# Another order of work from the softmax to the first expert in a hybrid encoder layer

## The chip, the cores and the metric

The kernel runs on one core of one Trainium2 chip. The metric is device time in microseconds (us) of one execution, lower is better. All engines of the core work side by side, each through its own list of instructions in order, and wait for one another with semaphores: PE (TensorE, matrix multiplication; PEld is its loading of weights), DVE (VectorE), ACT (ScalarE), POOL (GpSimd), and SP (SyncE), which only issues transfers from device memory.

## What is computed

One encoder layer over 256 tokens of width 1024: attention and a gated recurrence side by side, one output projection, then a mixture of 32 experts of which each token takes 4. All data are float32. Cut to what the change touches:

```python
mixed = jnp.concatenate([rms_norm(attn, attn_out_g[l]),
                         rms_norm(lru, lru_out_g[l])], axis=-1)
x = x + mixed @ w_out[l]                      # output projection, both halves
x = x + moe_ffn(rms_norm(x, norm2_g[l]), w_router[l], ...)
...
# moe_ffn
logits = (xf @ w_router + b_router)
top_v, top_i = lax.top_k(logits, TOP_K)       # 4 of 32
gates = jax.nn.softmax(top_v, axis=-1)
counts = jnp.bincount(flat_e, length=N_EXPERTS)
...
def expert_block(args):                       # rows of the tokens that chose expert e
    g = xb @ w_gate[e] + b_gate[e]
    u = xb @ w_up[e] + b_up[e]
    ...
    return ((u + 1.0) * glu) @ w_down[e] + b_down[e]
```

## The kernel before

The program has two parts, `front` (attention, recurrence, output projection, router) and `experts` (a loop over 32 experts). Nothing reorders the work: each engine runs its instructions in the order in which the Python code writes them, so the order of the code is the schedule.

The tokens stand in two tiles of 128 (t = 0, 1), the width of 1024 in halves of 512 (d = 0, 1). In the stretch at hand the code goes from the queries (`q_half`, `q_trans`) to the scores of the four pairs of token tile and key head (`scores`), their softmax (`score_exp` on DVE and ACT, `normalize` on DVE), the transposes of the probabilities (`p_trans` on PE, copied out by ACT in line L502), and their product with the values (`attend`). `attend_end`, `attend_sum`, `attend_ss` and `rms` make the attention's norm; L518 in `attend_end` writes `mT`, which the output projection reads.

The output projection is cut in eight pieces, `out_proj(p, half, t, d)`: half 1 is the recurrence, half 0 the attention, for each token tile t and output half d. Each piece is four matmuls of 128x512 into one bank of PSUM (L570), and `out_add` (DVE, L576) scales it and adds it to the residual `x1`. `x2_sq`, `x2_eps` and `x2_rstd` make the second norm; `x2_trans` and `x2_evac` transpose `x1`; `logits` multiplies with the router (L711); `choose` finds the four experts of each token (eight small DVE steps, L715 to L723) and leaves the choice in `sel`. Matmuls of `sel` with a triangle of ones (`upper`) and with ones give each token's place in its expert's list (`pk`, L762 to L765) and each expert's count (`pc`, L768). `open_acc` (PE, L726) writes `x1` into the PSUM bank in which the experts' results are summed.

PSUM has eight banks. Through the attention they are two pools of four, `pa` and `pf`; at `pctx.close()` the pool `pf` ends and the experts' pool (`pt_`) takes its banks, while the four `acc` banks are taken from `pa`.

`bias_split(h, i)` cuts the gate and up biases of all experts into three bfloat16 parts (ACT and POOL), which the experts' first matmuls read. `rms` needs another ACT function table than `exp` and `tanh`: a change of table is an ACT_TABLE_LOAD.

Each expert takes at most 64 tokens in its main path; when more chose it, `overflow` branches into extra blocks. So each of PE, DVE and ACT reads the expert's count from memory into a register (`load_cnt`, L937), gives PE a hint where the branch may go (L943), and branches on it (L868). For later experts this read stands in the middle of the expert before; for the first it stands right before its branch. Ahead of the branch stand `select`, `gather` (L812), `gather_trans` (L825, then the DVE step L826 that writes `xT`).

Weights come in pieces of 1 MB into a ring of 21 slots (`prefetch`, SP, L173), 12 pieces for an expert; a slot comes free when its last reader is done.

## Time and profile before

| | |
|---|---|
| median of three runs | 1096.49 us (1096.1 to 1096.49) |
| profiled execution: its own time, its span | 1097.01 us, 1095.2 us |
| PE busy in the span | 1046.3 us, 96% |
| first expert's first matmul (L831) starts | 138.94 us |
| last expert's last matmul (L934) starts its group | 1083.94 us |

Times in the rows below are us from the start of the span. In a row of the timeline, the number in square brackets is the time that the engine stood idle before the row, and behind the arrow what ended it. A float32 matmul shows as two records, so eight records of L570 are one piece of the output projection.

### The profile page before, as it was taken

What the parts mean: (1) busy time and instruction counts of PE and PEld (TensorE: products, weight loads), DVE (VectorE), ACT (ScalarE), POOL (GpSimd) and SP (SyncE); (2) the same over time, 40 slices, a digit from 0 to 9 for tenths busy, and PEclk for the clock granted to TensorE, in tenths of its full rate; (3) what the DMA queues carried; (4) which work ended last, traced back from release to release, by engine and by line L of the source; (5) the groups of instructions that cost most, each with busy time, mean ns of one, the idle gap of its engine ahead of it and who ended that gap; (6) DMA issues with size and microseconds to landing.
All of it is one profiled execution on the core that took longest, in us unless ns stands there. A gap on an engine that the chain in (4) does not pass through costs nothing. (4 is left out here: it accounts for less than half of the span.)

```text
span 1095.2 us, 12179 instructions
## 1 busy us (share of the span) xinstructions
PE 1046.3 (96%) x4802; PEld 439.8 (40%) x4802; DVE 246.4 (22%) x606; ACT 187.2 (17%) x343; POOL 16.5 (2%) x29
## 2 busy tenths in 40 slices
PE   9998799999999999989999998899999999999995
PEld 7865433333333333323343332233333333333331
DVE  5674312121212121211211121121212111112111
ACT  3746401011111111110011110011111111110112
POOL 1001100000000000000000000000000000000000
PEclk9999899999999999999999999899999999999998
DMA  9954579999999999999999999499999999999993
GB/s 323 406 193 155 235 303 413 421 420 420 419 420 421 419 420 420 420 421 390 413 421 420 420 420 422 169 401 422 419 420 420 420 420 420 419 420 419 421 421 138
DMA packets 65117, 419.10 MB, mean 383 GB/s; under 512 B 6664, under 2 KB 13968, under 8 KB 15984
## 3 DMA queue, kind: packets, MB, share of 16 engines
q1 hardware_dynamic: 64832, 417.22, 92.9%
q8 instruction: 72, 1.18, 0.4%
q0 software_dynamic: 176, 0.40, 0.1%
q14 instruction: 37, 0.30, 0.1%
HBM read 416.54 MB, written 1.05 MB: 381 GB/s over the span
## 5 line engine op out<-in xcount | busy, mean ns | idle before, releaser
L862 PE MATMUL pu<-w,gd 128*64 128x512 f32 x1024 | 228.9, 600 | 0.0
L835 PE MATMUL pu<-w,xT 128*64 128x512 f32 x1024 | 226.5, 593 | 1.7 <-DMA w<-in_w_up_dram 1.6
L835 PE MATMUL pg<-w,xT 128*64 128x512 f32 x1024 | 227.5, 596 | 0.0
L835 PEld LDWEIGHTS pu<-w,xT 128*64 128x64 f32 x1024 | 83.2, 137 | 133.0 <-issue 122.2
L835 PEld LDWEIGHTS pg<-w,xT 128*64 128x64 f32 x1024 | 84.3, 138 | 121.7 <-issue 115.0
L862 PEld LDWEIGHTS pu<-w,gd 128*64 128x64 f32 x1024 | 71.2, 138 | 144.3 <-issue 137.5
L841 DVE TENSOR_SCALAR gp<-pg 128x512 f32<-128x512 f32 x32 | 22.1, 692 | 297.5 <-PE pg L835 297.5
L1005 ACT ACTIVATE Y<-pu 64x512 f32<-64x512 f32 x60 | 35.5, 592 | 273.5 <-PE pu L862 273.1
L801 DVE TENSOR_SCALAR gd<-iota,pos,gates 128x64 f32<-128x64 f32 x128 | 30.1, 309 | 155.2 <-PEq L868 155.0
L812 PE MATMUL pt<-x,sr 128*64 128x512 f32 x256 | 61.5, 599 | 0.0
L842 ACT ACTIVATE sg<-gp 128x512 f32<-128x512 f32 x32 | 20.2, 630 | 240.9 <-DVE gp L841 240.9
L847 DVE TENSOR_SCALAR sg<-pu 128x512 f32<-128x512 f32 x34 | 23.5, 692 | 163.5 <-PE pu L835 163.3
L915 PE MATMUL ps<-Y,gT 128*128 128x512 f32 x120 | 54.0, 593 | 0.0
L815 ACT ACTIVATE sg<-pt 128x512 f32<-128x512 f32 x34 | 20.3, 598 | 140.5 <-PE pt L812 140.5
L826 DVE TENSOR_TENSOR xT<-pt,prm 128x512 f32<-128x512 f32 x32 | 22.1, 692 | 70.7 <-PE pt L825 70.7
L570 PE MATMUL ps<-w 128*128 128x512 f32 x64 | 28.8, 599 | 3.5 <-DVE w L518 2.5
L915 PEld LDWEIGHTS ps<-Y,gT 128*128 128x128 f32 x120 | 21.8, 192 | 21.5 <-issue 21.5
L812 PEld LDWEIGHTS pt<-x,sr 128*64 128x64 f32 x256 | 18.0, 136 | 29.2 <-issue 24.6
L296 PE MATMUL ps<-w 128*128 128x256 f32 x128 | 28.9, 386 | 0.0
L853 PEld LDWEIGHTS pt<-ident,gp 128*128 128x128 f32 x128 | 17.8, 208 | 27.6 <-DVE gp L848 14.6
L825 PE MATMUL pt<-ident,sg 128*128 128x128 f32 x136 | 25.2, 308 | 3.6 <-ACT sg L815 1.5
L843 DVE TENSOR_TENSOR gp<-gp,sg 128x512 f32<-128x512 f32 x32 | 22.2, 693 | 24.2 <-ACT sg L842 24.2
(255 smaller groups left out, 618.5 us busy)
## 6 DMA issues: line engine op xcount, KB each, us to landing
w<-in_w_gate_dram SPq DMA_DIRECT2D x128, 1024.0 KB, 19.8
w<-in_w_up_dram SPq DMA_DIRECT2D x128, 1024.0 KB, 19.8
w<-in_w_down_dram SPq DMA_DIRECT2D x127, 1024.0 KB, 19.8
w<-in_w_in_dram SPq DMA_DIRECT2D x6, 1024.0 KB, 11.6
w<-in_w_out_dram SPq DMA_DIRECT2D x4, 1024.0 KB, 11.9
x<-in_x_dram SPq DMA_DIRECT2D x2, 512.0 KB, 4.4
w<-in_w_in_dram SPq DMA_DIRECT2D x2, 512.0 KB, 7.1
w<-in_w_down_dram SPq DMA_DIRECT2D x2, 512.0 KB, 18.3
```

The source lines that it names most:

```text
L296: PE.matmul(p, lhsT=wi[i][:, k, cs], rhs=xT[:, k, :], start=k == 0, stop=k == KC - 1)
L570: PE.matmul(p, lhsT=mT[:, kk, t * 128:(t + 1) * 128], rhs=wo[kk // 2][:, kk % 2, d * 512:(d + 1) * 512], start=k == 0, stop=k == 3)
L801: V.tensor_scalar(dst[:, t], iota[:, b], pos[:, t, e:e + 1], weight[:, t], op0=OP.is_equal, op1=OP.mult)
L812: PE.matmul(p[h * 64:h * 64 + 64, :], lhsT=sl[:, t, :], rhs=x1[:, t, h * 512:(h + 1) * 512], start=t == 0, stop=t == NT - 1)
L825: PE.transpose(p[:, c].rearrange("p a b -> p (a b)"), column_pairs(xr, c), ident)
L826: V.tensor_tensor(dst.rearrange("p (h c) s -> p c h s", h=2), p, n2, OP.mult)
L835: PE.matmul(p[h * 64:h * 64 + 64, :], lhsT=xT[:, k, :], rhs=w[k // 2][:, k % 2, h * 512:(h + 1) * 512], start=False, stop=k == KC - 1)
L843: V.tensor_tensor(gp, gp, sg, OP.mult)
L847: V.tensor_scalar(u, p, LIMIT, -LIMIT, op0=OP.min, op1=OP.max)
L862: PE.matmul(p[q * 64:q * 64 + 64, :], lhsT=hT[:, c * 128 + hf * 64:c * 128 + hf * 64 + 64], rhs=w[j // 2][:, j % 2, d * 512:(d + 1) * 512] ...
L915: PE.matmul(acc[t][d], lhsT=gT[:, t, d, :], rhs=Y[d], start=False, stop=last)
L1005: S.activation(Y[q ^ (e % 2)][q * 64:q * 64 + 64, :], py[q * 64:q * 64 + 64, :], AF.Copy)
```

## The change

The work is the same, instruction for instruction, apart from two: the placing of tokens is done for each token tile (`place`) instead of for both at once. What moves:

- The square for the recurrence's norm, its sum (`pl_`), its square root and the two table loads stand ahead of the queries' transposes instead of behind them.
- The pieces of the output projection of half 1 are written one at a time between the softmax's steps, each with its own `out_add`, instead of two together. `normalize` of token tile 1 stands ahead of `attend` of tile 0.
- `p_trans` of token tile 1 stands ahead of the first piece of half 0; the other three pieces of half 0 stand among `attend` of tile 1, its norm, and the router.
- `bias_split` is spread over other places. Norm, transposes and logits of tile 0 come after the piece `out_proj(acc[1][0], 0, 1, 0)` instead of partly before it.
- The sums with `upper` and `ones` for tile 0 stand right after the second last piece; one `open_acc` instead of two stands ahead of `choose(1)`, two instead of one behind `gather`.
- The first expert's count is read before `gather` instead of after `gather_trans`.

Two adjacent `prefetch(1)` become one `prefetch(2)`; the transfers are the same in the same order.

```diff
+        S.activation(gt, gx, AF.Square)
         q_half(1, 0, pq1)
         q_half(1, 1, pq1)
-        S.activation(gt, gx, AF.Square)
...
-        pl0 = [out_proj(ps([128, 512], pa), 1, 0, d) for d in range(2)]
         pl_ = ps([128, NT], pf)
...
-        prefetch(1)
+        S.activation(ssl, pl_, AF.Sqrt, scale=1.0 / LW, bias=eps)
+        S.activation(e1, e1, AF.Tanh)
+        pl00 = out_proj(ps([128, 512], pa), 1, 0, 0)
         q_trans(0)
         q_trans(1)
-        prefetch(1)
-        S.activation(ssl, pl_, AF.Sqrt, scale=1.0 / LW, bias=eps)
-        S.activation(e1, e1, AF.Tanh)
+        prefetch(2)
...
-        for d in range(2):
-            out_add(pl0[d], ssl[:, 0:1], 0, d)
-        pl1 = [out_proj(ps([128, 512], pa), 1, 1, 0)]
+        out_add(pl00, ssl[:, 0:1], 0, 0)
+        pl01 = out_proj(ps([128, 512], pa), 1, 0, 1)
         ps11 = scores(1, 1, pf)
...
         prefetch(2)
-        normalize(1, 0, pb10)
-        normalize(1, 1, pb11)
         attend_end(0)
         at0 = attend_sum()
-        pa0 = [out_proj(ps([128, 512], pa), 0, 0, d) for d in range(2)]
+        bias_split(0, 0)
+        p_trans(pb10, pf)
+        p_trans(pb11, pf)
+        bias_split(1, 0)
+        pa0 = [ps([128, 512], pa) for d in range(2)]
+        out_proj(pa0[0], 0, 0, 0)
         attend_ss(0, at0)
         rms(ssa[:, 0:1], LW)
-        p_trans(pb10, pf)
-        p_trans(pb11, pf)
...
+        attend(1, 0, pb10)
+        attend(1, 1, pb11)
+        prefetch(3)
+        out_proj(pa0[1], 0, 0, 1)
+        out_add(pa0[0], ssa[:, 0:1], 0, 0)
+        attend_end(1)
+        at1 = attend_sum()
+        bias_split(0, 1)
...
+        pa1 = out_proj(acc[1][0], 0, 1, 0)
+        for kg in range(2):
+            x2_evac(x2_trans(0, kg), 0, kg)
+        out_add(pa1, ssa[:, 1:2], 1, 0)
+        x2_sq(1, 0)
+        bias_split(1, 1)
...
         choose(0)
+        x2_eps(1)
         pa1 = out_proj(acc[1][1], 0, 1, 1)
+        pk = pt_([128, NT, E], "pu", 1)
+        PE.matmul(pk[:, 0], lhsT=upper, rhs=sel[:, 0], start=True, stop=True)
+        PE.matmul(pk[:, 1], lhsT=ones, rhs=sel[:, 0], start=True, stop=False)
...
         logits(1, 1)
         open_acc(0, 0)
-        open_acc(0, 1)
...
         choose(1)
         PE.matmul(pk[:, 1], lhsT=upper, rhs=sel[:, 1], start=False, stop=True)
+        place(1)
...
-        open_acc(1, 0)
+        V.tensor_copy(cnti, pc)
+        open_acc(0, 1)
         prefetch(7)
...
         sl = select(0, 0)
+        cnt = load_cnt(0)
         xT = wk.tile([128, KC, 64], F32, name="xT")
         xr = gather(sl)
+        g["open_acc"](1, 0)
         g["open_acc"](1, 1)
         gather_trans(xr, xT)
         gate_norm()
...
-        cnt = load_cnt(0)
```

The order of the built programs at three places follows. First ACT between the last queries and the softmax's exponentials (L411 and L412 work on the queries, `qT` holds them transposed, `ssl` is the recurrence's norm, L484 is `exp`), before:

```order
L411 ACTIVATE w<-ps,rs_y_187 128x256
L412 ACTIVATE w<-w 128x256
L627 ACTIVATE w<-w 128x1024
L457 ACTIVATE qT<-ps 128x4x128 x2
L639 ACT_TABLE_LOAD
L639 ACTIVATE ssl<-ps,eps 128x2
L640 ACT_TABLE_LOAD
L640 ACTIVATE e_140<-e_140 128x8
L484 ACTIVATE w,sm<-ps,mx,rs_y_591 128x256 x12
```

and now:

```order
L411 ACTIVATE w<-ps,rs_y_187 128x256
L412 ACTIVATE w<-w 128x256
L634 ACT_TABLE_LOAD
L634 ACTIVATE ssl<-ps,eps 128x2
L635 ACT_TABLE_LOAD
L635 ACTIVATE e_140<-e_140 128x8
L457 ACTIVATE qT<-ps 128x4x128 x2
L484 ACTIVATE w,sm<-ps,mx,rs_y_591 128x256 x12
```

The two table loads moved from between the queries' copies and `exp` to ahead of the copies.

Second PE from `attend` of tile 0 to the first logits (L512 `attend`, L501 `p_trans`, L529 `attend_ss`, L696 `x2_trans`, L711 `logits`), before:

```order
L512 MATMUL ps<-w 64x128 x16
L570 MATMUL ps<-w 128x512 x8
L529 MATMUL ps<-ones,at_780 128x1
L501 MATMUL ps<-ident,w 128x128 x16
L512 MATMUL pu<-w 64x128 x16
L696 MATMUL pt<-ident,x_68 128x128 x8
L570 MATMUL ps<-w 128x512 x4
L529 MATMUL pg<-ones,at_871 128x1
L711 MATMUL pg<-wrb,w 128x32 x8
```

and now (L692 is `x2_trans`, L731 `logits`):

```order
L512 MATMUL ps<-w 64x128 x16
L501 MATMUL ps<-ident,w 128x128 x16
L570 MATMUL ps<-w 128x512 x4
L529 MATMUL ps<-ones,at_780 128x1
L512 MATMUL pu<-w 64x128 x16
L570 MATMUL ps<-w 128x512 x4
L529 MATMUL pg<-ones,at_857 128x1
L570 MATMUL ps<-w 128x512 x4
L692 MATMUL pt<-ident,x_68 128x128 x8
L731 MATMUL pg<-wrb,w 128x32 x8
```

Behind each `attend` and each norm now stands other PE work: the transposes or one piece of the projection.

Third PE from the last logits to the first branch, before:

```order
L711 MATMUL pg<-wrb,w 128x32 x8
L726 MATMUL ps<-x_68,ident 128x512 x2
L762 MATMUL pu<-sel,upper 128x32
L763 MATMUL pu<-sel,ones 128x32
L765 MATMUL pu<-sel,upper 128x32
L768 MATMUL pt<-sel,ones 1x32 x2
L726 MATMUL ps<-x_68,ident 128x512
L812 MATMUL pt<-x_68,sr 64x512 x4
L726 MATMUL ps<-x_68,ident 128x512
L825 MATMUL pt<-ident,sg 128x128 x4
L937 TENSOR_LOAD cnti
...
L868 COMPARE_AND_BRANCH
```

and now (L746 is `open_acc`, L774 and L778 the sums, L947 the count's read, L822 `gather`, L835 its transposes):

```order
L731 MATMUL pg<-wrb,w 128x32 x8
L746 MATMUL ps<-x_68,ident 128x512
L774 MATMUL pu<-sel,upper 128x32
L778 MATMUL pt<-sel,ones 1x32 x2
L746 MATMUL ps<-x_68,ident 128x512
L947 TENSOR_LOAD cnti
...
L1073 BRANCH_PREFETCH_HINT
L822 MATMUL pt<-x_68,sr 64x512 x4
L746 MATMUL ps<-x_68,ident 128x512 x2
L835 MATMUL pt<-ident,sg 128x128 x4
L878 COMPARE_AND_BRANCH
```

The read and the hint moved ahead of `gather`, one `open_acc` moved behind `choose(1)`'s sums and one behind `gather`, and two of the sums left this stretch.

## Rows read from the trace of the kernel before

**Rows 1.** The page's part 2: granted TensorE clock in 40 equal slices.

```profile
PEclk9999899999999999999999999899999999999998
```

**Rows 2.** Waits of PE, 66 to 140 us: us in total, times, longest.

```profile
PE pg L831 <- PEq L868: 4.5, 1, 4.5
PE pt L696 <- DVE x L576: 2.9, 1, 2.9
PE ps L570 <- DVE w L518: 2.5, 2, 1.3
PE ps L570 <- DVE x L576: 1.0, 1, 1.0
PE pu L512 <- ACT w L502: 0.8, 1, 0.8
PE ps L471 <- ACT ssl L639: 0.5, 1, 0.5
```

**Rows 3.** Timeline of PE: start, duration, what, idle before.

```profile
112.91 1.94 PE L711 MATMUL pg<-wrb,w 128*128 128x32 f32 x16 [0.30 <-issue]
114.69 3.68 PE L570 MATMUL ps<-w 128*128 128x512 f32 x8
...
122.22 3.00 PE L711 MATMUL pg<-wrb,w 128*128 128x32 f32 x16
125.03 3.76 PE L726 MATMUL ps<-x,ident 128*128 128x512 f32 x4
...
129.94 1.13 PE L726 MATMUL ps<-x,ident 128*128 128x512 f32 x2
...
138.94 0.41 PE L831 MATMUL pg<-b,emask 96*64 96x512 bf16 x2 [4.49 <-PEq L868]
139.15 8.76 PE L835 MATMUL pg<-w,xT 128*64 128x512 f32 x32
...
165.59 7.06 PE L835 MATMUL pg<-w,xT 128*64 128x512 f32 x32
```

**Rows 4.** Stretches: busy time of each engine, granted clock, DMA share, GB/s.

```profile
122.73:129.55 6.82, 6.82 (x23) 4.76 (x22) 1.98 (x10) 3.90 (x6) 0.54 (x2) 0.50 0.85 342
129.55:139.79 10.24, 5.75 (x28) 2.48 (x30) 2.67 (x10) 2.08 (x3) 0.00 (x0) 1.00 0.02 6
139.79:143.20 3.41, 3.41 (x10) 1.17 (x8) 0.00 (x0) 0.00 (x0) 0.00 (x0) 0.50 0.04 7
690.00:700.00 10.00, 9.00 (x34) 2.54 (x32) 0.00 (x0) 0.60 (x1) 0.00 (x0) 0.86 0.01 3
```

**Rows 5.** Timeline of ACT and DVE in the stretch that changes.

```profile
75.71 1.08 ACT L457 ACTIVATE qT<-ps 128x512 f32<-128x512 f32 x2 [6.42 <-PE ps L456]
76.81 1.28 ACT L639 ACT_TABLE_LOAD   x1
...
93.83 0.68 DVE L518 TENSOR_TENSOR w<-ps,prm 128x512 f32<-128x512 f32 x1
...
125.26 0.25 DVE L715 SCALAR_TENSOR_TENSOR lg<-pg,rstd,wrb 128x32 f32<-128x32 f32 x1 [2.08 <-PE pg L711]
...
126.77 0.19 DVE L723 TENSOR_TENSOR sel<-sel,eq 128x32 f32<-128x32 f32 x1
...
134.49 0.69 DVE L826 TENSOR_TENSOR xT<-pt,prm 128x512 f32<-128x512 f32 x1 [3.73 <-PE pt L825]
```

**Rows 6.** PE's count read and branch: count, duration in ns min/median/max, first and last start.

```profile
L937 PEldq TENSOR_LOAD <-cnti x32: 301/304/492, 133.7 to 1027.3; - x32
...
L868 PEldq COMPARE_BRANCH  x36: 90/352/3936, 134.8 to 1053.3; - x36
...
L868 PEldq COMPARE_BRANCH  x1: 2762/2762/2762, 160.8 to 160.8; - x1
```

**Rows 7.** Waits of PE, 139 to 1084 us: us in total, times, longest.

```profile
PE pg L831 <- PEq L868: 9.9, 31, 4.5
...
PE pu L835 <- DMA w<-in_w_up_dram: 1.6, 3, 0.6
```

More of the change, by code (lines that the diff above doesn't have):

```diff
@@ L653, in front @@
         p_trans(pb00, pf)
-        pl1.append(out_proj(ps([128, 512], pa), 1, 1, 1))
+        out_add(pl01, ssl[:, 0:1], 0, 1)
+        pl10 = out_proj(ps([128, 512], pa), 1, 1, 0)
         pb11 = score_exp(1, 1, ps11)
@@ L657, in front @@
         p_trans(pb01, pa)
-        for d in range(2):
-            out_add(pl1[d], ssl[:, 1:2], 1, d)
+        pl11 = out_proj(ps([128, 512], pa), 1, 1, 1)
+        normalize(1, 0, pb10)
+        out_add(pl10, ssl[:, 1:2], 1, 0)
+        normalize(1, 1, pb11)
+        out_add(pl11, ssl[:, 1:2], 1, 1)
         bias_load(0)
@@ L664, in front @@
         prefetch(2)
-        normalize(1, 0, pb10)
-        normalize(1, 1, pb11)
         attend_end(0)
         at0 = attend_sum()
-        pa0 = [out_proj(ps([128, 512], pa), 0, 0, d) for d in range(2)]
+        bias_split(0, 0)
[4 more added lines that the diff above has]
+        out_proj(pa0[0], 0, 0, 0)
         attend_ss(0, at0)
         rms(ssa[:, 0:1], LW)
-        p_trans(pb10, pf)
-        p_trans(pb11, pf)
-        bias_split(0, 0)
-        bias_split(1, 0)
-        for d in range(2):
-            out_add(pa0[d], ssa[:, 0:1], 0, d)
-            x2_sq(0, d)
-        x2_eps(0)
-        x2_rstd(0)
         pctx.close()
@@ L687, in pt_ @@
             return pe_.tile(shape, F32, name=tag, tag=tag, bufs=bufs)
-        acc = [[ps([128, 512], pa) for d in range(2)] for t in range(NT)][::-1]
-        g["psum"].update(ps=pt_, acc=acc)
+        acc = [[None] * 2 for t in range(NT)]
+        acc[1] = [ps([128, 512], pa) for d in range(2)]
         def x2_trans(t, kg):
@@ L700, in x2_evac @@
             V.tensor_copy(x2T[:, kg * 4:kg * 4 + 4, t * 128:(t + 1) * 128], p)
+        attend(1, 0, pb10)
[6 more added lines that the diff above has]
+        bias_split(0, 1)
+        x2_sq(0, 0)
+        out_add(pa0[1], ssa[:, 0:1], 0, 1)
+        x2_sq(0, 1)
+        acc[0] = [ps([128, 512], pa) for d in range(2)]
+        g["psum"].update(ps=pt_, acc=acc)
+        attend_ss(1, at1)
+        rms(ssa[:, 1:2], LW)
+        x2_eps(0)
+        x2_rstd(0)
+        pa1 = out_proj(acc[1][0], 0, 1, 0)
[4 more added lines that the diff above has]
+        bias_split(1, 1)
         lg = fr.tile([128, NT, E], F32, name="lg")
@@ L726, in open_acc @@
             PE.matmul(acc[t][d], lhsT=ident, rhs=x1[:, t, d * 512:(d + 1) * 512], start=True, stop=False)
-        attend(1, 0, pb10)
-        attend(1, 1, pb11)
-        prefetch(3)
-        attend_end(1)
-        at1 = attend_sum()
-        for kg in range(2):
-            x2_evac(x2_trans(0, kg), 0, kg)
-        pa1 = out_proj(acc[1][0], 0, 1, 0)
-        attend_ss(1, at1)
-        rms(ssa[:, 1:2], LW)
-        bias_split(0, 1)
-        bias_split(1, 1)
-        out_add(pa1, ssa[:, 1:2], 1, 0)
-        x2_sq(1, 0)
-        x2_eps(1)
         pl = pt_([128, NT, E], "pg", 1)
@@ L751, in front @@
         x2_sq(1, 1)
+        place(0)
         px = x2_trans(1, 1)
@@ L755, in front @@
         x2_rstd(1)
-        bias_split(0, 2)
-        bias_split(1, 2)
         logits(1, 1)
         open_acc(0, 0)
-        open_acc(0, 1)
-        pk = pt_([128, NT, E], "pu", 1)
-        PE.matmul(pk[:, 0], lhsT=upper, rhs=sel[:, 0], start=True, stop=True)
-        PE.matmul(pk[:, 1], lhsT=ones, rhs=sel[:, 0], start=True, stop=False)
         choose(1)
         PE.matmul(pk[:, 1], lhsT=upper, rhs=sel[:, 1], start=False, stop=True)
+        place(1)
         pc = pt_([1, E])
@@ L768, in front @@
             PE.matmul(pc, lhsT=ones[:, 0:1], rhs=sel[:, t], start=t == 0, stop=t == NT - 1)
[L769 removed]
+        V.tensor_copy(cnti, pc)
+        open_acc(0, 1)
         prefetch(7)
         g["open_acc"] = open_acc
[L773 to L774 removed]
+        bias_split(0, 2)
+        bias_split(1, 2)
         nm = fr.tile([128, NT, 1], F32, name="nm")
```

4 lines of the change are left out of this document (2 added, 2 removed).

## The prediction

> **What bounds the kernel now.** I read the page first, then the stretches, then the waits of PE, then single instructions. PE is busy for 96% of the span, so the question is which of its stretches contain time that is not work. From the first expert on there is little: between 139 and 1084 us PE waits 1.6 us in all for weights, and its largest entry, 9.9 us at the branches, holds the 4.5 us of the first one [rows 7], which leaves 5.4 us over 30 branches, 0.18 us each. The transfers could bind instead, but they run behind PE: in the 10 us around the start of the first expert they moved 6 GB/s, and from 690 to 700 us 3 GB/s, against 342 GB/s just before the first of these [rows 4]. With a ring of 21 slots that means that every slot was full both times, and a slot comes free only when PE has read it. So if PE starts the first expert earlier by some time, the stream of weights starts again earlier by the same time, and the end moves by the same time too. The place to cost is the time until 138.94 us, when the first expert's first matmul starts [rows 3].
>
> In the stretch ahead of it PE loses time in three ways. It waits: the six largest waits are 4.5 + 2.9 + 2.5 + 1.0 + 0.8 + 0.5 = 12.2 us [rows 2]. I leave out waits of 0.3 us, which both orders have. It runs at half clock: after the long wait of 2.9 us the granted clock is 0.50, that is 1.2 GHz instead of 2.4, from 122.73 to 129.55 us, and after the wait at the branch again from 139.79 to 143.20 us [rows 4]; digits under 9 on the page show the few later places [rows 1]. And it does its own work, which the change leaves as it is: the matmuls are the same ones in another order.
>
> **The change, term by term.** *The waits ahead of the first gather.* Five of the six waits, 7.7 us together, stand here, and for each I look at what PE has to do in its place now.
>
> The 2.5 us for L518 are two waits of `out_proj` for `mT`, which DVE writes in 0.68 us behind `attend` [rows 2, 5]. Now 16 transposes or a whole piece of the projection stand between. A piece is 3.68 us long at full clock [rows 3], five times what it has to cover: zero remains. The 0.8 us for ACT's copies of the transposed probabilities goes the same way: between them and `attend` of tile 1 stands a piece.
>
> The 1.0 us for the first `out_add` was a wait for a PSUM bank: two pieces and two score tiles held all four banks of `pa`. With one piece at a time the fourth bank is free. The 0.5 us at the scores was a bank whose reader, ACT, was still loading a table (1.28 us, and a second one behind it) [rows 2, 5]. Both loads now stand where ACT stood idle for 6.42 us ahead of the queries' copies [rows 5]: they cost nothing there, and the exponentials start earlier. If that cover were gone they would cost up to 2.6 us on ACT's list, but PE has pieces of the projection to do meanwhile.
>
> The 2.9 us was the transposes of tile 1 waiting for the last `out_add`, which on DVE stood behind `choose(0)`, which stood behind an epsilon step, which waited for ACT, which had two biases to round first. Now ACT has only one of them there, and the norm of tile 0 is done a piece of the projection earlier; `choose(0)`, 126.77 + 0.19 - 125.26 = 1.7 us by its twin [rows 5], fits into the 3.68 us of the last piece. Zero remains, or a few tenths.
>
> New waits come in. The transposes of the first probabilities now follow close on `normalize`: no row shows that, between 0 and 0.8 us (the wait of the same kind), I take 0.4. The logits of tile 0 follow directly on their own transposes, with a DVE copy of some 0.69 us (the same size as L826 [rows 5]) between, half of which the other four transposes cover: 0.2 to 0.7, I take 0.4. Behind the last logits PE has only one `open_acc`, about 1.0 us at full clock (1.13 us with its tail [rows 3]), to cover the 1.7 us of `choose(1)` and a step of waiting on each side: 0.7 to 1.2, I take 1.0. Fourth, the read of the count: it waits for the count, and behind it in PE's list stand `gather` and everything after. Its load took up to 0.49 us [rows 6] and the register steps and the hint about as much again; one `open_acc` is under way meanwhile, and DVE's `select` needs part of that time anyway: 0.3 to 1.1, I take 0.8. On DVE and ACT the same read stands where both wait for PE: nothing. Together 0.4 + 0.4 + 1.0 + 0.8 = 2.6 us (1.2 to 3.8). The term is 7.7 - 2.6 = 5.1 us gained.
>
> *The half clock before the gather.* It came after the wait of 2.9 us. Without a wait of that size I take it to be gone. Its price by twins at both clocks: the logits took 3.00 us against 1.94 us for tile 0, and two `open_acc` 3.76 us against 2 x 1.13 = 2.26 us [rows 3]: 1.06 + 1.5 = 2.6 us. Part of this time PE would now spend waiting for `choose(1)`, which is in the first term already.
>
> *The first branch.* PE stood 4.49 us ahead of L831 [rows 3]. Of that the DVE step L826 takes until 134.49 + 0.69 = 135.18 us, and 138.94 - 135.18 = 3.76 us stand behind it [rows 3, 5]: the load of the count, then a branch that took 3.94 us, against a median of 0.35 us [rows 6]. Now the hint is given ahead of `gather`, two `open_acc` and the transposes; the two `open_acc` alone are 2.26 us [rows 3], and the others bring it to about what the branch took. I take the branch as covered: what stays is L826 with its start (0.73 us) and the usual 0.18 us, 0.9 us together. Gain 4.5 - 0.9 = 3.6 us.
>
> *The first expert's first matmuls.* They took 8.76 us at partly half clock against 7.06 us for the second expert [rows 3]. With 0.9 us of waiting in place of 4.49 the clock should stay up: 1.7 us.
>
> *At nothing:* the moved bias rounding (ACT and POOL, long idle there; if late it would show as a wait of L831, which reads the third parts), the split of the placing into two DVE steps (under 0.25 us, and the first one is off the path), the one `open_acc` moved behind `gather` (work moved within PE's list; it hides ACT's copy of the gathered rows as the other one did), SP's transfers (same order; the slots come free earlier).
>
> The sum: 5.1 + 2.6 + 3.6 + 1.7 = 13.0 us. Against the profiled execution's own 1097.01 us that is 1084.0; the median lies 0.5 us under that execution, so 1083.5 us.
>
> **The rivals.** *The branch still stalls.* The second expert's branch took 2.76 us [rows 6], though its count had been read in the middle of the expert before. An early read did not make that branch short; PE's queued matmuls hid it. If the first branch does the same, it starts with the last transposes and lasts 2.76 to 3.94 us, of which some 0.5 us lie beside the transposes: PE waits 2.3 to 3.4 us instead of 0.9, and the half clock behind it stays (1.7). The gain shrinks to 13.0 - 1.7 - 1.4 to 2.5 = 8.8 to 9.9, so 1086.6 to 1087.7 us. For it: that one row. Against: the median of 0.35 us. The Trainium skill, page "Runtime: NRT & Kernel Launch", section "Instruction fetch mechanics", says that a taken branch to code outside the loaded pages waits for a transfer of that code, whatever the condition; by that rule it would be this rival, 1087 us, and the trace agrees as far as that 2.76 us goes, while most branches here, at 0.35 us, speak against it.
>
> *The clock falls anyway.* Between the last piece of the projection and the gather PE now has only short matmuls and transposes. If the half clock comes back there, the 2.6 us are not gained, and with a second stretch into the expert up to 1.7 more: 1086.1 to 1087.8 us. Against it: the waits there are about 1 us each, and a wait of 1.3 us for L518 [rows 2] drew no half clock before 122.73 us [rows 1, 4].
>
> *The weights bind.* If the stream did not start earlier with PE, the gain would be eaten at the places where PE waited 1.6 us for weights [rows 7], and the time would be within 2 us of 1096.5. The two stretches of 6 and 3 GB/s speak against it.
>
> *Slower.* The branch's code has moved in PE's list, and so for every later expert. The second branch started at 160.8 us and the next matmuls at about 165.4 us (0.2 us ahead of [rows 3]'s 165.59): 4.6 us of queued work hide it. If branches came to take more than that, each of 31 would cost the excess; from 4.6 + 13.0 / 31 = 5.0 us per branch the gain is gone, at 6 us the time would be 1083.5 + 31 x 1.4 = 1127 us. The longest so far is 3.94 us [rows 6].
>
> **How the numbers follow.** Forecast 0.58, branch 0.22, clock 0.14, weights 0.04, slower 0.02. The forecast's own bounds: the new waits 1.2 to 3.8 us give 1082.1 to 1084.7; the later half-clock places, three or four [rows 1], may each shrink or grow by one stretch worth up to 1.7 us, so I give 2 us either way for them, more to the low side as a shorter stretch could come twice. The range 1080 to 1088 us takes in the branch and the clock rival, and leaves out both together, the weights and the slow case. A measurement of this kernel can tell about 0.2% (2.2 us) from no change: faster 0.96, same 0.02, slower 0.02.
>
> **What would show it.** In the profile after, the first L841 (the expert's first matmul) should start near 127.7 us instead of 138.94 (5.1 + 2.6 + 3.6 earlier), with under 1.2 us ahead of it put down to the branch; the waits for `mT` and for the last `out_add` should be gone, and one of about 1 us at `choose(1)`'s sums and one at `gather` stand in their place; the granted clock should be 1.00 from 120 us into the first expert. Between that start and the end the time should shrink by the 1.7 us of the first expert alone. A first branch of 2.7 us or more makes the third term wrong, a 0.50 stretch ahead of the gather the second, and a longer wait for weights in the last experts the claim that the end moves along.

## The result, and the profile after

The changed kernel took 1083.2 us (median of 4 runs, 1080.3 to 1085.7) against 1096.3 for the kernel before (4 runs): a ratio of 0.989, 95% interval 0.985 to 0.992. The forecast was 1083.5. Both kernels were run again later beside the experiments. Over all runs the changed kernel has a mean of 1084.0 us (17 runs, 1078.0 to 1087.1) and the kernel before 1094.7 us (71 runs, 1089.8 to 1101.2). The typical gain is thus 10.7 us, with a 95% interval of about 1.5 either way, and not the 13.0 of the sum; the profiled execution of before lay 2.3 us above its kernel's mean.

The waits of PE in the stretch that [rows 2] shows for before (us in total, times, longest; 66 to 128 us here):

```profile
PE pg L841 <- DVEq L878: 1.4, 1, 1.4
PE pu L774 <- DVE sel L743: 0.9, 1, 0.9
PE pt L822 <- DVE sr L811: 0.6, 1, 0.6
PE pg L731 <- issue: 0.4, 1, 0.4
PE pu L512 <- DVE ssa L530: 0.3, 1, 0.3
...
PE pu L755 <- DVE ss L589: 0.3, 1, 0.3
PE pg L731 <- ACT w L763: 0.2, 1, 0.2
```

"After" is the changed kernel from here on. Its lines have moved: L841 and L845 are L831 and L835 of before (an expert's first matmuls), L878 is the branch, L811 `select`, L743 the last step of `choose`, L741 its scan, L755 the sums over `sel` of tile 0, L836 the DVE step that writes `xT`. PEq and DVEq stand for an engine's register and branch instructions.

The waits for `mT`, for the bank, for the table and for the last `out_add` are gone. In their place stand `choose(1)` (0.9), the gather (0.6), the logits of tile 0 (0.4), and three of 0.2 to 0.3. The timeline of PE, against [rows 3]:

```profile
118.08 0.41 PE L774 MATMUL pu<-sel,upper 128*128 128x32 f32 x2 [0.85 <-DVE sel L743]
...
120.33 1.94 PE L822 MATMUL pt<-x,sr 128*64 128x512 f32 x8 [0.57 <-DVE sr L811]
...
126.07 0.41 PE L841 MATMUL pg<-b,emask 96*64 96x512 bf16 x2 [1.42 <-DVEq L878]
126.31 7.04 PE L845 MATMUL pg<-w,xT 128*64 128x512 f32 x32
```

The first expert starts at 126.07 us instead of 138.94, and its first 32 matmuls take 7.04 us instead of 8.76. The stretches, against [rows 4] (us, then busy time of PE, PEld, DVE, ACT and POOL, granted clock, DMA share, GB/s):

```profile
90.00:120.00 30.00, 27.64 (x156) 17.01 (x152) 15.30 (x40) 18.52 (x31) 9.02 (x6) 1.00 0.74 287
120.00:126.00 6.00, 4.32 (x16) 1.88 (x16) 1.26 (x5) 2.08 (x3) 0.00 (x0) 1.00 0.49 203
126.00:129.60 3.60, 3.53 (x18) 1.29 (x20) 0.54 (x2) 0.00 (x0) 0.00 (x0) 1.00 0.15 20
```

In this execution no half clock is left ahead of the first expert or in it. From 128 us to the end the waits, against [rows 7]:

```profile
PE pg L841 <- PEq L878: 5.4, 30, 0.5
PE pu L845 <- DMA w<-in_w_up_dram: 2.0, 4, 0.6
...
PE pg L845 <- DMA w<-in_w_gate_dram: 0.4, 1, 0.4
```

The other branches cost what they did (0.18 us each). Waiting for weights rose from 1.6 to 2.4 us in this execution, so at most 0.8 us of the gain was given back there: but for that, the stream came along.

To set executions side by side I split each span at the same points: the end of the unchanged front (start of the first matmul behind the queries' part), the first expert's first matmul (L831 or L841), the second expert's first L835 or L845, and the end. The column "expert 0" is counted from the first expert's first L835 or L845, 0.2 us behind its first matmul, so a row adds up to 0.2 us less than its span. All in us, from the start times in each trace; the idle time is that of PE ahead of the first L831 or L841:

```
kernel, execution   front  front to expert 0  idle ahead  branch  expert 0  rest
before               66.4        72.5             4.5       3.9     26.4    929.6
after, 1st           65.7        60.3             1.4       1.9     24.7    929.6
after, 2nd           65.3        62.4             1.8       3.4     24.7    930.1
after, 3rd           65.5        60.8             1.9       3.4     24.7    925.0
e1_read_only         65.2        74.3             3.3       3.9     26.4    930.0
e4_bias_later        65.5        74.4             4.3       3.8     26.4    930.7
e13_one_bias         64.8        67.9             4.4       3.9     27.5    930.3
e3_tables_first      65.3        70.5             4.0       3.5     26.4    930.0
e2_late_read         65.3        63.2             3.4       3.7     26.0    924.9
e7b_more_work        65.2        67.7             2.4       3.9     24.7    926.2
e8_both              65.5        62.9             0.8       0.5     24.7    930.1
e10_no_hint          65.0        62.9             2.4       3.8     28.1    935.6
e9_branch_early      64.8        60.4             0.0       4.2     24.8    926.1
e11_early_bias       65.1        60.1             0.0       5.0     24.8    933.2
```

In the last two rows L841 stands ahead of the wait for `xT`, and L845 0.86 us behind it (in e9_branch_early), so their way and their idle time look better than they are: e9's first L845 stands 61.3 us behind the front, against 60.6, 62.6 and 61.0 in the three executions of after.

The profiled pair differs by 14.6 us: 0.7 in the unchanged front, 12.2 from there to the first expert, 1.7 in it, 0.0 in the rest.

### The profile page after: what moved, and what is told of

Same layout as the page of the kernel before. It is cut to its first block, busy times and chain, and to the rows that moved or that the text cites. A ratio compares the mean times of both kernels' runs of the same rounds, so it can differ in the third digit from the quotient of the medians.

```text
span 1080.6 us, 12185 instructions
## 1 busy us (share of the span) xinstructions
PE 1038.1 (96%) x4802; PEld 432.5 (40%) x4802; DVE 248.4 (23%) x607; ACT 187.0 (17%) x343; POOL 16.5 (2%) x29
## 5 line engine op out<-in xcount | busy, mean ns | idle before, releaser
L845 PE MATMUL pu<-w,xT 128*64 128x512 f32 x1024 | 226.5, 592 | 2.0 <-DMA w<-in_w_up_dram 2.0
L845 PE MATMUL pg<-w,xT 128*64 128x512 f32 x1024 | 227.7, 596 | 0.4 <-DMA w<-in_w_gate_dram 0.4
L845 PEld LDWEIGHTS pu<-w,xT 128*64 128x64 f32 x1024 | 82.6, 137 | 133.9 <-issue 121.3
L845 PEld LDWEIGHTS pg<-w,xT 128*64 128x64 f32 x1024 | 83.4, 137 | 123.2 <-issue 117.0
L811 DVE TENSOR_SCALAR gd<-iota,pos,gates 128x64 f32<-128x64 f32 x128 | 30.1, 310 | 151.8 <-PEq L878 151.7
L822 PE MATMUL pt<-x,sr 128*64 128x512 f32 x256 | 61.5, 599 | 0.6 <-DVE sr L811 0.6
L836 DVE TENSOR_TENSOR xT<-pt,prm 128x512 f32<-128x512 f32 x32 | 22.1, 692 | 71.6 <-PE pt L835 71.6
L822 PEld LDWEIGHTS pt<-x,sr 128*64 128x64 f32 x256 | 17.9, 136 | 29.9 <-issue 25.3
L863 PEld LDWEIGHTS pt<-ident,gp 128*128 128x128 f32 x128 | 17.8, 208 | 27.6 <-DVE gp L858 14.6
L835 PE MATMUL pt<-ident,sg 128*128 128x128 f32 x136 | 25.2, 308 | 3.6 <-ACT sg L825 1.5
## 6 DMA issues: line engine op xcount, KB each, us to landing
w<-in_w_in_dram SPq DMA_DIRECT2D x6, 1024.0 KB, 11.4
```

Of the source, the lines that this page charges most:

```text
L811: V.tensor_scalar(dst[:, t], iota[:, b], pos[:, t, e:e + 1], weight[:, t], op0=OP.is_equal, op1=OP.mult)
L822: PE.matmul(p[h * 64:h * 64 + 64, :], lhsT=sl[:, t, :], rhs=x1[:, t, h * 512:(h + 1) * 512], start=t == 0, stop=t == NT - 1)
L835: PE.transpose(p[:, c].rearrange("p a b -> p (a b)"), column_pairs(xr, c), ident)
L836: V.tensor_tensor(dst.rearrange("p (h c) s -> p c h s", h=2), p, n2, OP.mult)
L845: PE.matmul(p[h * 64:h * 64 + 64, :], lhsT=xT[:, k, :], rhs=w[k // 2][:, k % 2, h * 512:(h + 1) * 512], start=False, stop=k == KC - 1)
```

## The experiments

**The read of the count alone.** On the kernel before:

```diff
         sl = select(0, 0)
+        cnt = load_cnt(0)
         xT = wk.tile(...)
...
-        cnt = load_cnt(0)
         for e in range(E):
```

> The kernel before with one line moved: the count of expert 0 is read, and its hint given, right behind the first expert's select, ahead of its gather. Theory (the hint ahead of the transposes covers the branch): the compare and its code fetch run beside two open_acc and the transposes, PE's idle time ahead of the first L831 shrinks from 4.49 us to 0.7 to 1.5 us, the first L831 starts 3.0 to 3.8 us earlier less up to 1 us that the read itself may hold up the gather (some 2 to 3.6 us net), and the first expert's first matmuls fall from 8.76 towards 7.06 us if no half clock follows; the time is 2 to 5 us under the kernel before. Rival (a first branch stalls whatever the hint, as the second expert's with 2.76 us): the idle time ahead of L831 stays at 2.3 us or more, the half clock behind it stays, the time is 0.5 to 2 us under. The waits ahead of the gather stay as they were in both.

The time was 1096.97 us (10 runs), 1.0026 of before (0.9997 to 1.0054): no gain, and so in neither of the two ranges. Its wait and the stretch ahead of it:

```profile
PE pg L831 <- PEq L868: 3.3, 1, 3.3
```

```profile
120.20:133.80 13.60, 13.25 (x42) 8.27 (x44) 3.52 (x15) 4.83 (x8) 0.53 (x2) 0.50 0.55 217
```

The branch still took 3.87 us; it only began 0.14 us ahead of the transposes instead of behind them, so PE idled 1.2 us less. That is the rival's picture. In this execution the stretch at half clock ahead of it was 13.65 us long instead of 6.83, which took that and more away; whether that length is of the edit or of the one execution is not shown.

**The read put back late.** On the changed kernel, `cnt = load_cnt(0)` moved back to ahead of the expert loop:

> The changed kernel with one line moved back: the count of expert 0 is read behind the transposes, the normalisation of the gates and the sigmoid, as in the kernel before. Theory (the early read is what took the branch away): PE stands about 4.4 us ahead of the first matmul instead of 1.42, the first expert starts 2.4 to 3.1 us later than in the changed kernel (the 0.57 us wait ahead of the gather may go in exchange), a half clock may follow the wait and make the first matmuls up to 1.7 us longer: 3 to 5 us over the changed kernel, 1085.5 to 1088. Rival (the other edits brought the branch's cover, the read's place matters little): within 1 us of the changed kernel.

The idle time was 3.4 us where 4.4 was expected. A half clock of 3.41 us stood ahead of the gather in this execution, as in the second of after and in neither of the others, so the second is the fair one to compare with: the way to the first expert is 0.8 us longer than there and expert 0 1.3 us, 2.1 together. The trace bears the theory's direction out, at less than its size. The time does not show it: a mean of 1084.4 us (8 runs) against 1084.0, with 2.3 us of uncertainty, and not the 3 to 5 us of the theory. The profiled rest was as short as the shortest of after.

**The bias rounding, both biases.** On the kernel before both `bias_split(·, 1)` were moved to just ahead of `bias_split(·, 2)`:

> The kernel before with one edit: the second rounding steps of both biases (ACT and POOL) are moved from ahead of the tile 1 epsilon step to just ahead of the third ones. Theory (the 2.9 us wait of the tile 1 transposes came from ACT's two bias roundings ahead of the epsilon step, and the half clock from 122.7 us on came from that wait): the wait shrinks to under 1 us, the granted clock stays 1.00 until the branch, and the first L831 starts 4 to 5 us earlier; the time is 3.5 to 5.5 us under the kernel before. Rival 1 (the wait has another cause, such as choose(0) alone): the wait stays above 2 us and the time within 1 us. Rival 2 (the clock falls there anyway, since short matmuls and transposes follow): the wait goes, a stretch at 0.50 stays, and only about 2.5 us come.

The 2.9 us wait fell to 0.4, and no half clock followed it until 127.1 us, as the theory had it. But the time was 1097.46 us, 1.0031 of before (1.0005 to 1.0057), as a wait of 4.3 us appeared ahead of the gather. POOL and then DVE in this kernel:

```profile
124.48 2.12 POOL L547 TENSOR_TENSOR bl<-bl,b 32x1024 f32<-32x1024 f32 x1 [1.17 <-ACT b L546]
...
129.62 0.32 POOL L778 TENSOR_TENSOR gates<-gates,sel 128x64 f32<-128x64 f32 x1 [2.82 <-ACT gates L777]
```

```profile
129.97 0.54 DVE L800 TENSOR_SCALAR sr<-iota,pos,rstd 128x64 f32<-128x64 f32 x2 [4.72 <-POOL gates L778]
```

The late roundings on ACT and POOL stood in front of the gates, and `select` waits for the gates. A half clock (127.1, 6.83 us) came there instead.

**The bias rounding, one bias.** So the second bias alone, again on the kernel before:

```diff
         bias_split(0, 1)
-        bias_split(1, 1)
         out_add(pa1, ssa[:, 1:2], 1, 0)
         x2_sq(1, 0)
+        bias_split(1, 1)
```

> The kernel before with one line moved: the second rounding step of the second bias stands behind the square of tile 1's first half on ACT instead of ahead of it, as in the changed kernel; POOL's queue stays free for the gates. Theory (the 2.9 us wait came from ACT's second bias ahead of that square, by way of DVE's epsilon step and choose(0), and the half clock of 122.7 us came from that wait): the wait falls under 0.5 us, the other waits stay, the branch's 4.3 to 4.5 us stay, the gather comes 2.5 us earlier, and 4 to 5 us if the half clock goes as well; the time is 2.5 to 5 us under the kernel before. Rival 1 (choose(0) alone holds the transposes): over 1.5 us of the wait stay. Rival 2 (the clock falls anyway): a stretch at 0.50 still lies ahead of the gather, and 2.5 us come.

1088.76 us (8 runs), 0.9939 of before (0.9923 to 0.9956). The wait, and the stretches from the logits on:

```profile
PE pt L696 <- DVE x L576: 1.5, 1, 1.5
```

```profile
115.92 2.08 DVE L723 TENSOR_TENSOR sel<-sel,eq 128x32 f32<-128x32 f32 x1
```

```profile
122.00:131.80 9.80, 6.28 (x29) 2.83 (x27) 3.54 (x15) 3.69 (x6) 0.39 (x2) 1.00 0.52 215
131.90:138.70 6.80, 6.01 (x16) 2.11 (x18) 0.00 (x0) 0.00 (x0) 0.00 (x0) 0.50 0.11 22
```

Half of the wait went, and all of the half clock ahead of the gather. The way to the first expert is some 4.6 us shorter: 1.4 from the wait, 0.1 from the branch, and 3.2 in PE's busy time on it, 59.7 to 56.5 us, by the clock. The wait did not fall under 0.5 as expected, and not for the first rival's reason: the last step of `choose(0)`, shown above, took 2.08 us instead of the 0.19 of [rows 5], as it stood beside POOL's rounding, which ran from 115.83 to 117.95. Some 1.1 us of the wait is that; in e4_bias_later, where no POOL step stood beside `choose(0)`, 0.4 stayed. The half clock behind the branch is longer here (expert 0 takes 1.1 us more). One moved line gave about half of the change's gain: the mean is 5.8 us under that of before, with 2.3 of uncertainty.

**The tables alone.** On the kernel before, Square, the gated half's sums, Sqrt and Tanh were moved ahead of the queries' transposes, the pair of projection pieces behind them:

> The kernel before with only the tables' part of the change: the square, the sums of the gated half's norm, the square root and the hyperbolic tangent stand ahead of the queries' transposes, the two pieces of the output projection behind them as a pair. Theory (ACT idles there for over 6 us, so the two table loads of 1.28 us cost nothing, and the wait of 0.5 us at the scores goes): 0.5 us of waits go, at most 1.5; the exponentials start 3 to 5 us earlier; the time within 2 us of the kernel before. Rival (the loads delay the queries' copies): a wait for them of 1 to 2.6 us appears at the scores.

1094.29 us (10 runs), 0.9993 of before (0.9971 to 1.0014). The 0.5 us wait for the table is gone, no wait for the queries' copies came, and the wait for the bank grew from 1.0 to 2.0 us instead: with nothing else changed the saved time is handed to the next wait. The exponentials began 0.7 us earlier against the end of the front, where 3 to 5 was expected, since the pair of pieces now stands ahead of the transposes of the probabilities. (The way to the first expert is 2.0 us shorter in this execution, most of it by a half clock of 3.41 instead of 6.83 us at 123.0.)

**More work ahead of the first expert.** On the changed kernel the last piece of the projection is computed three times over into the same bank:

> The changed kernel with one piece of the output projection, behind choose(0), computed three times over into the same bank (the last one counts), so 2 x 3.68 = 7.4 us of matmuls more ahead of the first expert. Theory (the end moves one to one with the first expert's start, the stream of weights standing still until then): the first expert starts 7.0 to 7.4 us later (0.3 us of the wait behind choose(0) is covered) and the time grows by 6.5 to 7.7 us. Rival (the weights set the end, so an earlier start is given back later): the time grows by under 3 us, as waits for weights in the last experts shrink from 2.4 us to nothing, at most.

The first expert started 6.9 us later than in the first execution of after, and the mean time was 1089.7 us (10 runs), 5.7 us more than after with 2.4 us of uncertainty, where 6.5 to 7.7 was expected. Under 3 us is excluded; what is put ahead of the first expert moves the end.

**Gate norm ahead, second bias later.** On the changed kernel:

```diff
         x2_sq(1, 0)
-        bias_split(1, 1)
...
+        bias_split(1, 1)
         bias_split(0, 2)
...
+        gate_norm()
         gather_trans(xr, xT)
-        gate_norm()
```

> The changed kernel with two edits. The normalisation of the gates (three DVE steps) stands ahead of the first gather's transposes instead of behind; the second rounding step of the second bias (ACT, POOL) stands behind choose(1) instead of ahead of choose(0). Theory 1 (DVE's scan in choose(0) took 2.19 us instead of 0.28 because POOL worked on the bias at the same time): the scan takes 0.3 us again, and PE's two waits of about 0.3 us around the sums of tile 0 go. Rival: the scan stays at 2.2 us. Theory 2 (DVE reached its branch late because of the normalisation): PE's 1.4 us ahead of the first expert shrink to 0.8 to 1.0 us. Rival (PE's own branch sets it): if the branch takes 3.7 us or more, PE idles 2 us or more, whatever DVE does. Together 0.5 to 1.1 us less than the changed kernel, which is less than these runs can tell.

What led to it is a step in the changed kernel that no row of before has. DVE and POOL there:

```profile
109.77 2.19 DVE L741 TENSOR_TENSOR_SCAN pre<-ones,need,eq 128x32 f32<-128x32 f32 x1
...
117.29 0.28 DVE L741 TENSOR_TENSOR_SCAN pre<-ones,need,eq 128x32 f32<-128x32 f32 x1
```

```profile
109.77 2.12 POOL L547 TENSOR_TENSOR bl<-bl,b 32x1024 f32<-32x1024 f32 x1 [6.93 <-ACT b L546]
```

With the rounding moved, both scans took 0.28 us, and another step stood still beside POOL:

```profile
115.52 2.11 POOL L547 TENSOR_TENSOR bl<-bl,b 32x1024 f32<-32x1024 f32 x1 [12.89 <-ACT b L546]
```

```profile
116.14 1.55 DVE L737 TENSOR_TENSOR sel<-lg,m 128x32 f32<-128x32 f32 x1
```

Now `choose(1)` was late, and PE waited 2.2 us for it instead of 0.9; a half clock followed, ahead of the first expert:

```profile
118.20:125.00 6.80, 6.27 (x16) 1.96 (x16) 1.93 (x10) 2.33 (x4) 0.32 (x1) 0.50 0.59 249
```

So the collision is real, and the edit moved it to a dearer place. The idle time ahead of the first expert was 0.84 us: the branch took only 0.51 us in this execution, its code having been fetched from 122.91 us on, 3.0 us ahead of it, and DVE's norm was out of the way; the run does not part the two. The time was 1084.4 us (6 runs), as after's.

**The branch ahead of the transposes.** On the changed kernel `overflow(cnt, 0, ...)` and `gate_norm()` stand ahead of the first `gather_trans`, and the first gathered rows have a buffer of their own:

> The changed kernel with the first expert's branch ahead of the first gather's transposes, right behind the two open_acc; the gathered rows lie in a buffer of their own, and the normalisation of the gates stands ahead of the branch. Theory (PE's sequencer can take the branch while the two open_acc are still running, and the branch takes some 3.8 us from the moment at which it is reached, hint or not): the branch starts 1.5 to 2.5 us earlier, at 120.6 to 121.5 us, ends at 124.4 to 125.3, the transposes and DVE's xT follow within 1.6 us, and the first expert starts at 126.0 to 127.0 us: 0 to 1 us earlier than in the changed kernel if its branch takes 3.8 us there, about the same if it takes 1.9. Rival (the sequencer cannot run ahead of two open_acc): the branch starts only when they end, at 124, and the first expert 2 to 3 us later.

PE's timeline (an idle of 0.30 us behind the branch, and 0.45 for DVE's `xT`):

```profile
122.21 1.98 PE L746 MATMUL ps<-x,ident 128*128 128x512 f32 x4
124.50 0.72 PE L835 MATMUL pt<-ident,gT 128*128 128x128 f32 x4 [0.30 <-PEq L878]
...
126.00 7.09 PE L845 MATMUL pg<-w,xT 128*64 128x512 f32 x32 [0.45 <-DVE xT L836]
```

The branch began at 119.4 us, earlier than expected, and took 4.2 us beside the gather and both `open_acc`, so little of it was left to wait for. A half clock of 3.41 us stood ahead of the gather (117.7). The time was 1080.47 us (6 runs), 0.9864 of before (0.9832 to 0.9897), beside after's 0.9902.

**With the second bias ahead, too.** The same with `bias_split(1, 1)` right behind `x2_rstd(0)`:

> The kernel e9_branch_early with the second rounding step of the second bias moved ahead, to just behind the inverse norm of tile 0 on ACT, so that POOL's subtraction runs at about 104.5 to 106.6 us, before choose(0) begins. Theory (a DVE step that reads two operands from SBUF stands still while POOL's subtraction runs; ACT is idle there for 3.7 us): both scans take 0.3 us, no DVE step of choose(0) or choose(1) takes over 0.3 us, PE's wait for tile 0's sums (0.25 to 0.3 us) goes, and the first expert starts 0.3 to 0.6 us earlier at an equal clock; the time is 0 to 1 us under e9_branch_early's, less than these runs can tell. Rival (the long scan has another cause): the scan takes 2.2 us wherever POOL works.

```profile
104.71 2.12 POOL L547 TENSOR_TENSOR bl<-bl,b 32x1024 f32<-32x1024 f32 x1 [2.53 <-ACT b L546]
```

```profile
109.13 0.28 DVE L741 TENSOR_TENSOR_SCAN pre<-ones,need,eq 128x32 f32<-128x32 f32 x1
```

No DVE step of `choose` is long any more, and the wait for tile 0's sums is gone. The branch took 5.0 us and PE waited 1.5 us for it, so the start is no earlier. 1083.17 us (6 runs), 0.9882 (0.9861 to 0.9902). The two kernels with the early branch have a mean of 1081.6 us (12 runs), 2.4 us under after with 1.8 us of uncertainty: probably a little faster than both kernels, by less than one of them alone can show.

**Without the first four hints.**

> The changed kernel without the branch hint for the first four experts; the counts are read at the same places, the other 28 hints stay. Theory (for the first experts' branches the hint does not bring the code; the branch fetches it when it is reached): the first three branches take 2.6 to 3.9 us as before, and the time is within 1 us of the changed kernel. Rival 1 (the hint brings the code): the first branch takes 0.5 us or more longer than in the changed kernel run beside it. Rival 2 (the hint gets in the way): the branches become shorter. Four instructions go, so the code that follows lies at other addresses, which may by itself change a branch's length.

1087.82 us (12 runs), a mean 4.4 us over after (2.0 of uncertainty). The first branch took 3.81 us, 0.4 more than the 3.37 in the execution of after that ran beside it, which is less than the first rival wanted. For the next three experts the theory failed, and that is where the hint counted; the second and third:

```profile
L878 PEldq COMPARE_BRANCH  x2: 6072/6087/6102, 149.7 to 176.8; - x2
```

The fourth took 5.64 us. In the first execution of after these three took 2.66, 2.77 and 0.36. The two of 6.1 us made PE wait 1.8 us each, and ahead of the fourth expert it waited 1.4 us, which the profile puts down to DVE. The time rose by more than the 1 us of the theory. Four instructions fewer also move the code that follows, and e7b_more_work shows that moved code can change which branches are long, though none was over 3.9 us there; the run does not part the hint from that. In this execution a half clock of 6.83 us also stood ahead of the gather (114.8).

**The changed kernel again.** Twice, unchanged:

> The changed kernel once more, on the chip and beside the runs of the three that follow. It asks which parts of its profile are of the program and which of the one execution. Theory (the first branch's length is set by where its code lies in memory, which is the same in each run of one program): the first branch takes 1.8 to 2.1 us again, with its code fetch starting ahead of it, and PE idles 1.4 us ahead of the first L841. Rival (it was chance): the branch takes 3.7 to 3.9 us, as in the four other kernels profiled so far, and PE idles about 2.4 us. The stretches at half clock in the first two experts are absent in both; those in the last two experts may differ.

> The changed kernel once more, beside e11_early_bias on one chip. It asks again what is of the one execution: the first branch took 1.93 us in one profile and 3.37 us in another of the same program. Theory (whether the hint has started the code's fetch before the branch is reached differs from run to run): the branch takes 0.5 to 2 us, or 3.3 to 3.9 us, and its fetch starts before the branch in the first case and some 1 us behind the branch's start in the other; PE idles 1.4 to 1.9 us ahead of the first L841 either way. Rival (the fetch has nothing to do with it): the length does not go with the fetch.

1085.51 us (6 runs, 0.9902 of before) and 1085.22 us (7 runs, 0.9904). PE's first branch in the three executions, the first one first (count, then ns min/median/max and start):

```profile
L878 PEldq COMPARE_BRANCH  x1: 1933/1933/1933, 123.0 to 123.0; - x1
```

```profile
L878 PEldq COMPARE_BRANCH  x1: 3371/3371/3371, 124.2 to 124.2; - x1
```

```profile
L878 PEldq COMPARE_BRANCH  x1: 3392/3392/3392, 122.8 to 122.8; - x1
```

In the first the fetch of the code (16 KB on the instruction queue) began at 122.49, 0.5 us ahead of the branch; in the others 0.96 and 0.98 us behind its start. In all three the branch ended some 1.5 us after that fetch had landed. So the length goes with the fetch, as the theory of e12_after_third had it, and it is not fixed by where the code lies, as that of e0_after_again had it. The idle time of 2.4 us that went with the long branch there did not come either: 1.8 and 1.9. The second execution also had a half clock ahead of the gather:

```profile
120.20:123.60 3.40, 3.40 (x9) 0.85 (x6) 0.00 (x0) 0.09 (x1) 0.00 (x0) 0.50 0.50 210
```

## Why the prediction was right

*The bound.* The end moved with the first expert's start, as the prediction read from the two empty stretches of the stream: between profiles of before and after the rest is 929.6 us in both. That equality is partly luck, as before lost 3.4 us at half clock near 215 us and after the same in its last expert (42.2 us instead of 38.8). The fairer pair is before and the second execution of after: four later half-clock stretches each, every one some 12.8 us earlier in after (488.0 and 475.1 us, say), and a rest of 929.6 and 930.1. And e7b_more_work pushed the end from the other side.

*The waits ahead of the gather.* 7.7 us were to become 2.6, and became 0.85 + 0.57 + 0.39 + 0.28 + 0.25 + 0.3 = 2.6. Before had a wait of 0.30 at the first logits too [rows 3], which the prediction booked as wholly new, so what was gained is 5.4 us rather than the 5.1 forecast. Within the 2.6, `choose(1)` (0.9 for 1.0) and the first logits (0.4) were sized well. So was the gather (0.6 for 0.8), but its cause as the profile has it is not the read of the count: PE waits for `select`, and `select` for the gates on POOL, which stand behind ACT's third roundings of the biases and a change of table:

```profile
119.51 0.54 DVE L811 TENSOR_SCALAR sr<-iota,pos,rstd 128x64 f32<-128x64 f32 x2 [0.60 <-POOL gates L789]
```

The read and its hint were through at 120.0 us, the same time as `select`, so no run parts the two. The wait at the transposes behind `normalize` did not come, and three small ones were not foreseen. One of them, 0.28 us at tile 0's sums, is what is left of DVE's scan standing still for 1.9 us beside POOL, which the 3.68 us piece covered. The claim that the moved rounding costs nothing on POOL was too easy: it held by that cover.

*The half clock.* Right for the profiled execution, too strong as a rule. PE's busy time on the way to the first expert fell from 59.7 to 55.9 us. Of these 3.8 us the stretch at half clock accounts for 3.4: [rows 4] has PE busy for 6.82 of its 6.83 us, and half of that is lost. The prediction's 2.6 priced only the logits and two `open_acc` by their twins. But the wait does not fix the stretch. Behind the same wait of 2.9 us it lasted 6.83 us in before, 13.65 in e1_read_only and 3.41 in e3_tables_first. And of six executions whose work up to there is that of the changed kernel (three of after, e2, e9, e10), four had one ahead of the first expert: 3.41 us in three of them, 6.83 in e10. So "gone" is not what the runs show, and the clock rival came true in part. Losing half of each stretch, that is 3.9 us on average against 1.4, a term of about 2.5 (an estimate from these nine profiles): the size was nearly right, by way of two errors.

*The branch.* Right in its size, wrong in its reason. The early hint was to cover it; it still takes 3.4 us in two executions of three, and 3.7 to 5.0 in six other kernels, with an early hint, a late one or none; only e8_both, in its one profile, has it short, with the fetch 3.0 us ahead. The rival had this: the row of 2.76 us told the truth about the first experts. The median of 0.35 us came from experts whose code had been fetched some microseconds ahead of the branch (in after, for the fourth expert, the fetch at 197.6 and the branch at 204.3 us), and said nothing of the first. What brought the gain is that the branch now starts when ACT's copy of the gathered rows is ready, 1 us ahead of the transposes, and runs beside them and DVE's `xT`. The early read alone put it 0.14 us ahead (e1_read_only); the rest came with the `open_acc` that now stands behind `gather`. PE idled 1.4, 1.8 and 1.9 us, where 0.9 was forecast and 2.3 to 3.4 by the rival. In the first execution the last to come was not PE's branch but DVE:

```profile
124.69 0.69 DVE L836 TENSOR_TENSOR xT<-pt,prm 128x512 f32<-128x512 f32 x1 [4.63 <-PE pt L835]
...
125.74 0.22 DVE L920 TENSOR_TENSOR gates<-gates,gs 128x64 f32<-128x64 f32 x1
```

Three steps of the gates' norm lie behind `xT`, and DVE's own side of the branch behind them, at 126.0 us. The Trainium skill, page "Runtime: NRT & Kernel Launch", section "Instruction fetch mechanics", says that a taken branch to code outside the loaded pages waits for a transfer of that code. The trace agrees: in every run here each branch of 1.9 us or more has a fetch of code that starts inside it or 0.5 us ahead of it, and the ones of 0.35 us have theirs earlier, so these do not speak against the rule, as the prediction had it. The section says nothing of a hint, so the prediction's "whatever the condition" goes beyond it; without the hints the second and third branch took 6.1 us, with two fetches inside each.

*The first expert.* 24.7 us instead of 26.4 in all three executions of after: the 1.7 us forecast. The early read alone did not bring it (26.4 in e1_read_only).

*The sum.* The three executions need 60.3, 62.4 and 60.8 us from the front to the first expert, a mean of 11.4 less than before; the sum had 11.3. By PE's idle and busy time, as a mean of the three, that is 5.4 from the waits (5.1 forecast), 2.8 from the branch (3.6) and 3.2 from the clock (2.6): misses of 0.3, -0.8 and 0.6 that cancel. So all three terms are there, and the sum is better than they are, which is luck. So is part of the hit on the total. The kernels' means lie 10.7 and not 13.0 apart: the sum started from an execution 2.3 us above its kernel's mean, while the three profiled ones of after lie 2.4 us under theirs (mean 1081.6). Part of that can lie behind the first expert, where the rest is 925 to 930 us in executions of one and the same program. At about 202 us a stretch at 0.50 of 6.83 us stood in the second execution and none in the other two (3.4 us lost), and the last expert takes 38.8 or 42.2 us in the same way. Before had four such later stretches, of which [rows 1] shows two as digits under 9 behind the first. Why the clock falls there in one execution and not in the next is open.

## What to carry over

Price a stretch at half clock by PE's busy time in it, half of which is lost, and not by the two groups that have a twin; and price it over several profiles, as its length differs between executions with the same work. Ask what wait stands ahead of it: one line that shortened one wait gave 4.6 us ahead of the first expert. When a step is moved, write down what stands behind it and beside it on every engine that it uses: both roundings of the biases, on ACT and POOL ahead of the gates, made PE wait 4.3 us, and one of them beside `choose(1)` made it wait 2.2 us instead of 0.9. A median over many branches says nothing about the first ones; look at the first alone.

## What the runs showed of the hardware

**A DVE step with two operands in SBUF stands still while POOL's subtraction runs.** A scan took 2.19 instead of 0.28 us, ending with POOL's step of 2.12 us; a TENSOR_TENSOR 1.55 instead of 0.19, another 2.08 (e13_one_bias), a third 1.28 (e4_bias_later). Moved away from POOL, the scan and the steps of `choose` were short. The Trainium skill, page "SBUF — State Buffer", section "Who interferes with whom", has the rule: such a DVE step contends with a GpSimd step that reads SBUF. All runs here agree: each long one ended within 0.1 us of POOL's subtraction.

**The first three branches are unlike the later ones.** They took 1.9 to 3.4, 2.6 to 2.9 and 2.7 to 2.8 us in the changed kernel's three executions, all later ones 0.5 us or less. With 16 records of matmuls more in the program (e7b_more_work) the second and third took 0.37 us, and five of the last took 3.3 to 3.8, all hidden. Where a branch was short, no fetch of code began inside it: the second one of e7b_more_work began at 153.10 us, and the fetch before it at 144.75. A fetch ahead is not enough by itself, as the fourth branch without a hint had one 10.2 us ahead and took 5.64 us. Why the fetch starts ahead of the branch in one execution and behind the branch's start in another is open.
